# A feed-forward up projection by block products: seven per pair of feature tiles where there were eight, with the gated values kept in DRAM

## The chip, the cores and the metric

The program runs on one core of a Trainium2 chip. The core has a matrix engine (TensorE, PE in the profile), three engines for elementwise work (VectorE or DVE, ScalarE or ACT, GpSimd or POOL), an engine that only issues transfers (SyncE, SP), and 16 DMA engines between its on-chip memory (SBUF) and DRAM. TensorE writes to eight accumulator banks (PSUM), which ACT and DVE read. The metric is the device time of one execution in microseconds (us).

## The reference

Two blocks of a network on 1024 tokens of 1024 features, float32. The part that the change touches is the gated feed-forward layer of the first block, with 2816 hidden features:

```
def conv_glu_ffn(h, w_up, conv_w, w_down):
    up = causal_dwconv(h @ w_up, conv_w)
    ...
    return (jax.nn.silu(gate) * val) @ w_down
```

Here `h` is the normalised input (1024 tokens by 1024 features), `w_up` has 5632 columns (2816 for the gate, then 2816 for the value), `causal_dwconv` is a convolution of three taps along the tokens for each feature, and `w_down` brings 2816 features back to 1024.

## The kernel before

Every float32 operand of a product is split in two parts: `hi`, the rounded value in TensorE's fast format (a cast on ACT, L100), and `lo`, the rest (a subtraction on DVE or GpSimd, L101). A product is then three: hi by hi, hi by lo, lo by hi. The helper `split` writes both parts, `wload` (L103) loads 128 columns of a weight into the tile `wraw` (two buffers) and splits them, and `mm3` multiplies (L123).

The up projection works on 22 pairs of feature tiles (`NF` = 22, 128 features each). A pair is one gate tile and the value tile of the same number; here it is called a unit. For each of the two tiles of a unit the kernel loads 512 KB of weights, splits them, and issues 8 (slices of the 1024 inputs) x 3 (parts) x 2 (halves of the tokens) = 48 products of 128x128 by 128x512: 96 for the unit, 2112 in all. The sums of a tile lie in a PSUM tile `mm` of two banks, one bank for each half of the tokens. `up_evict` (L1030 to L1036) reads it: ACT takes the last tap, DVE the other two (L1034, L1035). Then come tanh on ACT (L1055), two products on DVE (L1056, L1060), and the gated values stay in SBUF, in the tiles `slots`, for the down projection. A new `wraw` can be filled when its older contents are split, so SP's transfer waits for DVE's subtraction.

The down projection (L1165 to L1167) runs in four passes: for each half of the tokens (`j`) and each half of the 1024 output features (`c`) it takes 22 steps, and a step multiplies one 128x512 tile of `w_down` and one of the gated values, split on the way, in 12 products.

A scheduler in the compiler orders the instructions of every engine by priorities and estimated lengths; pools with few buffers set what waits for what. What the scheduler made of the code is shown below with the change.

## Time and profile before

| | us |
|---|---|
| three timed executions | 2518.94, 2516.62, 2511.92 |
| their median | 2516.62 |
| the profiled execution: span from first to last instruction | 2505.2 |
| output projection and norm, from 1020 | 1020.0 to 1110.7 |
| up projection | 1110.7 to 1593.2 |
| down projection | 1593.2 to about 1842 |
| second block | 1842 to 2505.2 |

The span is what the rows below are counted in; the time of an execution also has a start and an end in it, and the median stands 11.4 us above the span (the profiled execution's own time is not listed beside the three). A row of the profile's table of windows gives, for each engine, its busy time and the number of its instructions in that stretch; "PEclk" is the clock that TensorE was granted, as a share of full speed. A busy PE is not the same as a PE that does new work at its full rate, since matmuls are pipelined: the time from the start of one matmul to the start of the next is the price of one.

### The profile page before, as it was taken

To read this page: it belongs to the slowest core of one execution; us is meant where nothing else is said; L and a number is where in the kernel's file an instruction comes from. 1 tells how busy PE (TensorE), PEld (TensorE's weight loads), DVE (VectorE), ACT (ScalarE), POOL (GpSimd) and SP (SyncE) were. 2 spreads that over 40 slices of the span, in tenths; PEclk is the share of its full clock that TensorE was granted. 3 is DMA by queue.
4 is the path that set the end of the run, shared out by engine and by line. 5 is a ranking of instruction groups with operands and counts; after the bars stand their busy time and mean duration, and the time that the engine had idled before them with its cause. 6 is when DMAs were issued, how large, how long until landed. Compare 5 with 4: busy or idle time off the path is not lost.

```text
span 2505.2 us, 31186 instructions
## 1 busy us (share of the span) xinstructions
PE 2396.7 (96%) x11582; PEld 1942.4 (78%) x11582; DVE 1322.8 (53%) x2247; ACT 992.9 (40%) x1869; POOL 356.4 (14%) x477
## 2 busy tenths in 40 slices
PE   6999999997999999999999999999999999999999
PEld 5777777776777777788788888888889787777787
DVE  4244754677554333444444444456665534668852
ACT  4333433222343122323222222345556633669840
POOL 0122320112231211000000000000013200125510
...
GB/s 150 101 88 78 43 58 164 147 147 83 88 119 65 166 153 168 206 77 51 53 50 43 51 51 47 114 97 135 163 125 83 143 179 175 197 187 183 127 107 138
DMA packets 272056, 288.10 MB, mean 115 GB/s; under 512 B 13968, under 2 KB 208160, under 8 KB 271904
## 3 DMA queue, kind: packets, MB, share of 16 engines
...
## 4 chain that ended last, share of the span: by engine, by line
PE 47%; DMA 6%; ACT 3%; DVE 3%; issue 1%; SPq 0%; POOL 0%; POOLq 0%; ACTq 0%; DVEq 0%
PE mm L123 19%; PE ip L1219 3%; DMA mr<-merged 2%; PE tp L330 1%; PE iq L314 1%; PE ip L1108 1%; PE ip L1109 1%; PE ip L1110 1%; PE lt L1503 1%; PE iq L315 1%; ACT p L1507 1%; DMA wr<-in_w_in_dram 1%; PE ho L1503 1%; DMA zr<-in_w_in_dram 1%; PE iq L1109 1%
## 5 line engine op out<-in xcount | busy, mean ns | idle before, releaser
L100 ACT CAST whi<-wraw 128x1024 fp32r<-128x1024 f32 (+1 forms) x138 | 121.8, 883 | 524.8 <-PE mm L123 499.7
L101 DVE TENSOR_TENSOR wlo<-wraw,whi 128x1024 fp32r<-128x1024 f32 (+1 forms) x138 | 143.8, 1043 | 345.6 <-ACT whi L100 341.6
L123 PE MATMUL mm<-hh,whi 128*128 128x512 f32 x896 | 306.4, 413 | 6.0 <-ACT th L846 5.1
L123 PE MATMUL mm<-hl,whi 128*128 128x512 f32 x896 | 293.7, 399 | 0.0
L123 PE MATMUL mm<-hh,wlo 128*128 128x512 f32 x896 | 291.7, 397 | 1.3 <-DVE wlo L115 1.3
L123 PE MATMUL mm<-h2l,whi 128*128 128x512 f32 x704 | 222.4, 389 | 0.0
L123 PE MATMUL mm<-h2h,wlo 128*128 128x512 f32 x704 | 222.0, 389 | 0.0
L123 PE MATMUL mm<-h2h,whi 128*128 128x512 f32 x704 | 222.0, 389 | 0.0
L123 PEld LDWEIGHTS mm<-hh,wlo 128*128 128x128 f32 x896 | 170.6, 191 | 39.2 <-DVE wlo L115 1.9
L123 PEld LDWEIGHTS mm<-hl,whi 128*128 128x128 f32 x896 | 170.3, 191 | 37.2 <-issue 1.0
L123 PEld LDWEIGHTS mm<-hh,whi 128*128 128x128 f32 x896 | 160.9, 192 | 42.1 <-ACT th L846 6.4
L123 PEld LDWEIGHTS mm<-h2l,whi 128*128 128x128 f32 x704 | 132.1, 188 | 28.6 <-issue 1.3
L123 PEld LDWEIGHTS mm<-h2h,whi 128*128 128x128 f32 x704 | 132.1, 188 | 27.9 <-ACT whi L100 0.6
L123 PEld LDWEIGHTS mm<-h2h,wlo 128*128 128x128 f32 x704 | 132.2, 188 | 27.4
L167 POOL TENSOR_TENSOR rs<-rs,negh 128x1 f32<-128x1 f32 x32 | 19.4, 610 | 868.7 <-ACT junk L164 602.9
L1507 ACT ACTIVATE p<-p,mn 128x640 f32<-128x640 f32 (+7 forms) x128 | 99.5, 778 | 12.6 <-DVE mn L1505 12.2
L101 DVE TENSOR_TENSOR gl<-s,gh 128x512 fp32r<-128x512 f32 x87 | 59.8, 689 | 65.4 <-ACT gh L100 62.9
L101 DVE TENSOR_TENSOR ptl<-tp,pth 128x512 fp32r<-128x512 f32 (+3 forms) x144 | 77.9, 554 | 30.7 <-ACT pth L100 29.4
L100 ACT CAST gh<-s 128x512 fp32r<-128x512 f32 x87 | 53.9, 621 | 79.7 <-PE iq L1166 32.7
L100 ACT CAST pth<-tp 128x512 fp32r<-128x512 f32 (+3 forms) x144 | 66.9, 477 | 43.5 <-PE tp L330 42.3
L314 PE MATMUL iq<-pth,v 128*128 128x512 f32 x192 | 70.8, 370 | 9.9 <-ACT pth L100 4.9
L856 POOL TENSOR_TENSOR acc<-acc,pacc 128x1024 f32<-128x1024 f32 x20 | 49.3, 2464 | 186.5 <-DVE acc L851 133.0
...
## 6 DMA issues: line engine op xcount, KB each, us to landing
wraw<-in_w_in_dram SPq DMA_DIRECT2D x60, 512.0 KB, 3.9
wraw<-in_w_up_dram SPq DMA_DIRECT2D x44, 512.0 KB, 3.8
wr<-in_w_down_dram SPq DMA_DIRECT2D x87, 256.0 KB, 2.6
merged<-acc SPq DMA_DIRECT2D x28, 512.0 KB, 2.9
pacc<-merged SPq DMA_DIRECT2D x20, 512.0 KB, 3.9
x<-x ACTq DMA_DIRECT2D x16, 512.0 KB, 2.8
v2t<-vo ACTq DMA_DIRECT2D x16, 512.0 KB, 2.6
v<-v2t SPq DMA_DIRECT2D x16, 512.0 KB, 4.0
```

The lines of the kernel that those rows point to most:

```text
L100: S.copy(hi, src)
L101: (eng or V).tensor_tensor(lo, src, f(hi), op=ALU.subtract)
L123: PE.matmul(ps[:, c0 + j * 512:c0 + (j + 1) * 512], w[:, k, :], x[j][:, k, :], start=(k == 0 and w is wh and x is xh), stop=(k == nkt - 1 ...
L314: PE.matmul(po[-1][:, w], vh[:, k, :], ph_[:, w], start=(k == 0), stop=False)
L315: PE.matmul(po[-1][:, w], vh[:, k, :], pl_[:, w], start=False, stop=(k == nk - 1))
L330: PE.transpose(pt[:, i * 128:(i + 1) * 128], P[p0 + i][:, k * 128:(k + 1) * 128], ident)
L856: G.tensor_tensor(ac, ac, pa, op=ALU.add)
L1108: PE.matmul(ps[:, :ncol], xh[:, k, :], wh[:, :ncol], start=(k == 0), stop=False)
L1109: PE.matmul(ps[:, :ncol], xh[:, k, :], wl[:, :ncol], start=False, stop=False)
L1219: PE.matmul(ps[j], w[:, k, :], x[j][:, n, :], start=(n == 0 and w is wh and x is hh), stop=(n == 7 and bool(last)))
L1503: PE.matmul(ps[:, 0:c1 - c0], a[:, i * 128:(i + 1) * 128], b[:, c0:c1], start=(n == 0), stop=(n == len(self.passes) - 1))
L1507: S.activation(pr_[:, :L], pr_[:, :L], AF.Exp, scale=-1.0, bias=mn[:, c:c + 1], accum_out=self.den[:, i:i + 1])
```

## The change

The normalised input, turned (features by tokens), is seen as four blocks: two halves of the features by two halves of the tokens. A unit's weights are four blocks as well: two halves of the inputs by gate and value. The product of such 2x2 blocks takes eight block products; Strassen's algorithm (here in Winograd's form) takes seven and some more additions. `Unit.p1` to `Unit.p7` are the seven, 4 slices x 3 parts = 12 matmuls each, 84 for a unit and 1848 in all.

- On the side of the tokens, the sums of blocks are made once (lines L1181 to L1197 of the new kernel): `B1` (two blocks as they are), `T1` to `T4` and `B22`, from the raw transposes that `NormBlocks` keeps; each of `T1` to `T4` and `B22` is 128x2048 and split in `hi` and `lo`.
- On the side of the weights, four sums of 128x512 are made for each unit on GpSimd (`sums`, L1070 to L1073), from both `wraw` tiles. They make two tiles `s12` and `s34` of 128x1024, each split (`pair`) into `uhi` and `ulo`. The gate's weights are split as before (`w1`), and of the value's only the lower half (`w4`, 128x512).
- The products of one unit are added up in two accumulator banks of one `mm` tile (`a` and `c`) and one bank of `ip` (`d`). What several outputs share is read out between products: `e1` (ACT's copy of `a` after `p1`), `u2` and `e15` (DVE). The gate's and value's columns before the convolution are now in SBUF (`cg`, `cx`): `c11` is ACT's copy of `a`, the other three quarters are DVE additions (L1134, L1138, L1142). The convolution (`conv`) reads these.
- The last product of the gate is made on GpSimd (L1159, 128x1024), and the result is written to DRAM (`gg_d`, 512 KB for a unit). The down projection loads it again in its first two passes, 44 tiles of 256 KB (L1337).
- The small tables of the second block, which stood in the fifth turn of the loop, stay in the fifth (`n == 4`). Pools change sides; outside the feed-forward layer every engine runs the same instructions in the same order.

The diff, cut to its core:

```diff
+    class NormBlocks(Norm):
+        def __init__(self, pool, psum, gain, parts, raws):
+            super().__init__(pool, psum, gain, None, None)
+            self.parts, self.raws = parts, raws
+        def turn(self, t, xn):
+            j, c = divmod(t, 4)
+            s = slice(c * 128, (c + 1) * 128)
+            for q in range(2):
+                pt = self.psum.tile([128, 512], F32, name="tp", bufs=2).rearrange("p (a b) -> p a b", a=4)
+                for i in range(4):
+                    PE.transpose(pt[:, i, :], xn[q][:, i * 128:(i + 1) * 128], ident)
+                S.copy(self.raws[q, j][:, :, s], pt)
+                if j == 0:
+                    hi, lo = self.parts[q]
+                    split(hi[:, :, s], lo[:, :, s], self.raws[q, j][:, :, s])
...
+    gg_d = dram.tile([NF * 128, T], F32, name="gg")
+    stu = ExitStack()
+    up = None
+    def halves4(x):
+        return x[:, 0:4, :], x[:, 4:8, :]
+    class Unit:
+        def __init__(self, fi):
+            self.fi = fi
+        def load(self):
+            self.raw = [wpool.tile([128, NK, 128], F32, name="wraw") for _ in range(2)]
+            for i in range(2):
+                c = (i * NF + self.fi) * 128
+                nc.sync.dma_start(self.raw[i], A["w_up"][:, c:c + 128].rearrange("(k p) c -> p k c", p=128))
+        def w1(self):
+            hi = wpool.tile([128, NK, 128], F32R, name="whi")
+            lo = wpool.tile([128, NK, 128], F32R, name="wlo")
+            split(hi, lo, self.raw[0])
+            (self.a11, self.a12) = zip(halves4(hi), halves4(lo))
+        def sums(self):
+            (a11, a12), (a21, a22) = map(halves4, self.raw)
+            x = up.tile([128, 2, 4, 128], F32, name="s12")
+            y = up.tile([128, 2, 4, 128], F32, name="s34")
+            G.tensor_tensor(x[:, 1], a21, a22, op=ALU.add)
+            G.tensor_tensor(x[:, 0], x[:, 1], a11, op=ALU.subtract)
+            G.tensor_tensor(y[:, 0], a11, a21, op=ALU.subtract)
+            G.tensor_tensor(y[:, 1], a12, x[:, 0], op=ALU.subtract)
+            self.x, self.y = x, y
+        def pair(self, x):
+            hi = up.tile([128, 2, 4, 128], F32R, name="uhi", bufs=2)
+            lo = up.tile([128, 2, 4, 128], F32R, name="ulo", bufs=2)
+            split(hi, lo, x)
+            return (hi[:, 0], lo[:, 0]), (hi[:, 1], lo[:, 1])
+        def w2(self):
+            self.s2, self.s1 = self.pair(self.x)
+        def w3(self):
+            self.s3, self.s4 = self.pair(self.y)
+        def w4(self):
+            hi = wpool.tile([128, NK, 128], F32R, name="whi")[:, 0:4, :]
+            lo = wpool.tile([128, NK, 128], F32R, name="wlo")[:, 0:4, :]
+            split(hi, lo, self.raw[1][:, 4:8, :])
+            self.a22 = hi, lo
+        def product(self, acc, w, x, start):
+            (wh, wl), (xh, xl) = w, x
+            for k in range(4):
+                for n, (a, b) in enumerate(((wh, xh), (wh, xl), (wl, xh))):
+                    PE.matmul(acc, a[:, k, :], b[:, k, :], start=(start and k + n == 0), stop=(k == 3 and n == 2),
+                              skip_group_check=True)
+        def banks(self):
+            ps = mmp.tile([128, T], F32, name="mm")
+            self.a, self.c = ps[:, 0:512], ps[:, 512:1024]
+        def p1(self):
+            self.product(self.a, self.a11, B1[0], True)
+            self.e()
...
+        def e(self):
+            self.e1 = up.tile([128, 512], F32, name="e1", bufs=2)
+            S.copy(self.e1, self.a)
+        def p2(self):
+            self.product(self.a, self.a12, B1[1], False)
+        def c11(self):
+            self.g = up2.tile([128, T], F32, name="cg")
+            S.copy(self.g[:, 0:512], self.a)
+        def p6(self):
+            self.product(self.c, self.s2, T2, True)
+            self.u2 = up.tile([128, 512], F32, name="u2")
+            V.tensor_tensor(self.u2, self.c, self.e1, op=ALU.add)
+        def p5(self):
+            self.d = ipx.tile([128, 512], F32, name="ip", bufs=2)
+            self.product(self.d, self.s1, T1, True)
+            self.e15 = up.tile([128, 512], F32, name="e15")
+            V.tensor_tensor(self.e15, self.d, self.e1, op=ALU.add)
+        def p7(self):
+            self.product(self.c, self.s3, T3, False)
+            self.v = up2.tile([128, T], F32, name="cx")
+            V.tensor_tensor(self.v[:, 512:1024], self.c, self.e15, op=ALU.add)
+        def p3(self):
+            self.product(self.d, self.s4, B22, False)
+            V.tensor_tensor(self.g[:, 512:1024], self.d, self.u2, op=ALU.add)
+        def p4(self):
+            self.product(self.c, self.a22, T4, False)
+            V.tensor_tensor(self.v[:, 0:512], self.c, self.e1, op=ALU.add)
+        def conv(self, x, w):
+            a = up2.tile([128, T], F32, name="cv", bufs=3)
+            S.activation(a, x, AF.Copy, scale=w[2])
+            V.scalar_tensor_tensor(a[:, 1:T], x[:, 0:T - 1], w[1], a[:, 1:T], op0=ALU.mult, op1=ALU.add)
+            V.scalar_tensor_tensor(a[:, 2:T], x[:, 0:T - 2], w[0], a[:, 2:T], op0=ALU.mult, op1=ALU.add)
             return a
-        for fi in range(NF):
...
-                    mm3(ps[i], *w2[i], hh, hl, NK)
-                    cv_.append(up_evict(ps[i], i * NF + fi))
...
+        def gate(self):
+            a = self.conv(self.g, [PV("ffn_conv_w", 2 * NF * i + self.fi) for i in range(3)])
+            self.th = up2.tile([128, T], F32, name="th")
+            S.activation(self.th, a, AF.Tanh, scale=0.5)
+            V.scalar_tensor_tensor(self.th, self.th, 1.0, a, op0=ALU.add, op1=ALU.mult)
+        def value(self):
+            b = self.conv(self.v, [vw[:, NF * i + self.fi:NF * i + self.fi + 1] for i in range(3)])
+            G.tensor_tensor(b, self.th, b, op=ALU.mult)
+            nc.sync.dma_start(gg_d[self.fi * 128:(self.fi + 1) * 128, :], b)
+    us = [Unit(fi) for fi in range(NF)]
+    us[0].load()
+    us[0].w1()
+    us[0].banks()
+    us[0].product(us[0].a, us[0].a11, B1[0], True)
+    last_turn()
+    sto.close()
+    up = stu.enter_context(tc.tile_pool(name="up", bufs=1, side="right", reuse_waits="tile"))
+    vw = up.tile([128, 3 * NF], F32, name="vw")
+    tc.keep_in_program_order(V.tensor_scalar(vw.rearrange("p (i f) -> p i f", i=3),
+                                             PV("ffn_conv_w", 0, 6 * NF).rearrange("p (i e f) -> p i e f", i=3, e=2)[:, :, 1, :],
+                                             0.5, None, op0=ALU.mult))
+    tpool = stu.enter_context(tc.tile_pool(name="tpool", bufs=1, side="right", reuse_waits="tile"))
+    T4, T1, T2, T3, B22 = [[tpool.tile([128, 4, 512], F32R, name=f"{n}{e}") for e in "hl"] for n in ("t4", "t1", "t2", "t3", "b2")]
+    us[0].e()
+    us[0].p2()
+    us[0].sums()
+    us[0].w2()
+    V.tensor_tensor(R2[0, 0], R2[0, 1], R2[0, 0], op=ALU.subtract)
+    split(*T1, R2[0, 0])
+    split(*B22, R2[1, 1])
+    G.tensor_tensor(R2[0, 1], R2[1, 1], R2[0, 1], op=ALU.subtract)
+    us[0].w4()
+    us[1].load()
+    us[1].w1()
+    us[1].banks()
+    us[1].p1()
+    us[1].p2()
+    V.tensor_tensor(R2[1, 1], R2[1, 1], R2[0, 0], op=ALU.subtract)
+    split(*T2, R2[1, 1])
+    us[0].p5()
+    us[0].w3()
+    V.tensor_tensor(R2[1, 0], R2[1, 0], R2[1, 1], op=ALU.subtract)
+    split(*T3, R2[0, 1])
+    split(*T4, R2[1, 0])
+    str_.close()
+    up2 = stu.enter_context(tc.tile_pool(name="up2", bufs=1, reuse_waits="tile"))
+    us[0].c11()
+    us[1].sums()
+    us[0].p6()
+    us[1].w2()
+    us[0].p3()
+    us[0].gate()
+    us[0].p7()
+    us[1].w3()
+    us[0].p4()
+    us[0].value()
+    us[1].w4()
+    us[2].load()
+    us[1].p5()
+    us[1].c11()
+    us[1].p6()
+    us[2].w1()
+    us[2].sums()
+    us[1].p3()
+    us[1].gate()
+    us[1].p7()
+    us[2].w2()
+    us[1].p4()
+    us[1].value()
+    us[2].w3()
+    for n in range(2, NF):
+        u, v = us[n], us[n + 1] if n < NF - 1 else None
+        u.banks()
+        u.p1()
+        u.w4()
+        if v:
+            v.load()
+        u.p6()
+        if n == 4:
+            with tc.tile_pool(name="tb", bufs=1) as tb:
+                block2_tables(tb)
+        u.p5()
+        u.p2()
+        u.c11()
+        if v:
+            v.w1()
+            v.sums()
+        u.p7()
+        if v:
+            v.w2()
+        u.p3()
+        u.gate()
+        u.p4()
+        u.value()
+        if v:
+            v.w3()
...
+                    if j == 0:
+                        g_ = f(slot(c))
+                        nc.sync.dma_start(g_, gg_d[fi * 128:(fi + 1) * 128, c * 512:(c + 1) * 512])
+                        gg.setdefault(fi, {})[c] = g_
+                    raw = dw.tile([128, 512], F32, name="wr", bufs=3)
+                    nc.sync.dma_start(raw, A["w_down"][fi * 128:(fi + 1) * 128, c * 512:(c + 1) * 512])
+                    wh, wl, gh, gl = [dw.tile([128, 512], F32R, name=name, bufs=2) for name in ("dwh", "dwl", "gh", "gl")]
+                    with tc.high_priority():
+                        split(wh, wl, raw)
+                        split(gh, gl, gg[fi][j])
```

What the scheduler makes of it is shown at three places. The first is a unit in the middle of the up projection, on ACT and on GpSimd. ACT before (`whi` the cast of a weight tile, `cv` the first tap of the convolution, `th` tanh):

```order
L100 CAST whi_9859<-wraw_9857 128x1024
L1033 ACTIVATE cv_9840<-mm_9739,pv_63 128x1024
L100 CAST whi_9978<-wraw_9976 128x1024
L1033 ACTIVATE cv_9913<-mm_9863,pv_63 128x1024
L1055 ACTIVATE th_9969<-cv_9913 128x1024
```

ACT after, from the copy `e1` of unit n (its PSUM tile is mm_9793) to the copy `e1` of unit n+1:

```order
L1111 COPY e1_9806<-mm_9793 128x512
L100 CAST uhi_9883<-s12_9863 128x1024
L100 CAST whi_9859<-wraw_9812 128x1024
L1118 COPY cg_9857<-mm_9793 128x512
L100 CAST uhi_9926<-s34_9864 128x1024
L1146 ACTIVATE cv_9900<-cg_9857,pv_63 128x1024
L100 CAST whi_9945<-wraw_9813 128x512
L1146 ACTIVATE cv_9920<-cx_9881,vw_8203 128x1024
L1154 ACTIVATE th_9904<-cv_9900 128x1024
L1111 COPY e1_9943<-mm_9930 128x512
```

Five instructions for each unit have become nine, and `c11` of unit n (L1118) stands behind two casts that belong to unit n+1 (`uhi` of `s12`, and `whi`). The product `p7` of unit n waits for that copy, since `a` and `c` lie in one tile and the wait is placed for the tile. GpSimd, which has no instruction of the feed-forward layer before, has these for the same unit (wraw_9812 and wraw_9813 are the weights of unit n+1, cv_9783 is the value of unit n-1):

```order
L1070 TENSOR_TENSOR s12_9863<-wraw_9813 128x512
L1159 TENSOR_TENSOR cv_9783<-th_9767,cv_9783 128x1024
L1071 TENSOR_TENSOR s12_9863<-s12_9863,wraw_9812 128x512
L1072 TENSOR_TENSOR s34_9864<-wraw_9812,wraw_9813 128x512
L1073 TENSOR_TENSOR s34_9864<-wraw_9812,s12_9863 128x512
```

The product with the gate (L1159) stands between the first and the second sum of the next unit's weights.

The second place is DVE at the start of the up projection. Before, there stand (after the last splits of the norm) the small tables and the first unit:

```order
L101 TENSOR_TENSOR wlo_8305<-wraw_8302,whi_8304 128x1024
L1034 SCALAR_TENSOR_TENSOR cv_8287<-mm_8189,pv_63,cv_8287 128x1023
L1035 SCALAR_TENSOR_TENSOR cv_8287<-mm_8189,pv_63,cv_8287 128x1022
L1056 SCALAR_TENSOR_TENSOR th_8295<-th_8295,cv_8287 128x1024
L101 TENSOR_TENSOR wlo_8311<-wraw_8308,whi_8310 128x1024
```

After, the operands `T1` to `T4` and `B22` (names t1l to t4l, b2l, and the raw blocks r00 to r11) are made there:

```order
L101 TENSOR_TENSOR ulo_8306<-s34_8233,uhi_8305 128x1024
L1181 TENSOR_TENSOR r00_7415<-r01_7416,r00_7415 128x2048
L101 TENSOR_TENSOR b2l_8217<-r11_7418,b2h_8216 128x2048
L101 TENSOR_TENSOR t1l_8211<-r00_7415,t1h_8210 128x2048
L101 TENSOR_TENSOR wlo_8257<-wraw_8252,whi_8256 128x1024
L1191 TENSOR_TENSOR r11_7418<-r11_7418,r00_7415 128x2048
L101 TENSOR_TENSOR t3l_8215<-r01_7416,t3h_8214 128x2048
L101 TENSOR_TENSOR t2l_8213<-r11_7418,t2h_8212 128x2048
L1129 TENSOR_TENSOR e15_8303<-ip_8290,e1_8218 128x512
L1195 TENSOR_TENSOR r10_7417<-r10_7417,r11_7418 128x2048
L101 TENSOR_TENSOR wlo_8402<-wraw_8253,whi_8401 128x512
L101 TENSOR_TENSOR t4l_8209<-r10_7417,t4h_8208 128x2048
```

Eight subtractions of 128x2048 stand ahead of the second unit's work; the small tables follow them.

The third place is SP at the end of the up projection. Before, the transfers of the down projection's weights stand behind the last loads of the up projection, and one of them (L1064) between:

```order
L107 DMA wraw_10732<-in_w_up_dram 128x8x128
L1064 DMA wraw_10851<-in_w_down_dram 128x512
L107 DMA wraw_10864<-in_w_up_dram 128x8x128
L107 DMA wraw_10870<-in_w_up_dram 128x8x128
L1153 DMA wr_11023<-in_w_down_dram 128x512
```

After (gg is the buffer in DRAM, cv_11272 the gated values of the last unit, x2 the rows of the residual, s0 the tiles that the down projection reads):

```order
L1340 DMA wr_11358<-in_w_down_dram 128x512
L1364 DMA x2_11840<-x1_7408 128x1024
L1364 DMA x2_11842<-x1_7408 128x1024
L1340 DMA wr_11382<-in_w_down_dram 128x512
L1364 DMA x2_11844<-x1_7408 128x1024
L1340 DMA wr_11406<-in_w_down_dram 128x512
L1160 DMA gg_8164<-cv_11272 128x1024
L1364 DMA x2_11846<-x1_7408 128x1024
L1337 DMA s0_11305<-gg_8164 128x512
L1337 DMA s0_11329<-gg_8164 128x512
```

The first load of gated values (the tile of unit 0) stands in the queue behind the store of the last unit's.

## Rows read from the trace of the kernel before

**Rows 1.** The profile's table of windows, by stage.

```profile
core 0: us, PE busy (x) PEld busy (x) DVE busy (x) ACT busy (x) POOL busy (x), PEclk, DMA share, GB/s
1020.00:1110.70 90.70, 84.61 (x390) 67.48 (x389) 43.20 (x64) 29.91 (x57) 3.86 (x7) 1.00 0.42 140
1110.70:1593.20 482.50, 482.50 (x2127) 397.38 (x2126) 219.83 (x214) 117.46 (x119) 0.55 (x1) 1.00 0.16 48
1593.20:1842.00 248.80, 247.26 (x1092) 201.02 (x1091) 155.96 (x246) 129.05 (x244) 6.59 (x9) 1.00 0.43 139
```

**Rows 2.** The waits of the up projection: engine, line, waited for; us, times, longest.

```profile
ACT whi L100 <- PE mm L123: 276.3, 41, 11.7
DVE wlo L101 <- ACT whi L100: 213.3, 41, 6.7
```

**Rows 3.** The timeline of PE inside a unit: start, us, what, count.

```profile
1200.07 0.62 PE L123 MATMUL mm<-h2l,whi 128*128 128x512 f32 x2
...
1202.34 0.62 PE L123 MATMUL mm<-h2h,whi 128*128 128x512 f32 x2
```

**Rows 4.** The timeline of the other engines around one weight tile.

```profile
1288.33 1.05 ACT L100 CAST whi<-wraw 128x1024 fp32r<-128x1024 f32 x1 [4.90 <-PE mm L123]
1289.28 1.11 ACT L1033 ACTIVATE cv<-mm,pv 128x1024 f32<-128x1024 f32 x1
1289.42 1.23 DVE L101 TENSOR_TENSOR wlo<-wraw,whi 128x1024 fp32r<-128x1024 f32 x1 [4.73 <-ACT whi L100]
1290.56 1.28 DVE L1034 SCALAR_TENSOR_TENSOR cv<-mm,pv,cv 128x1023 f32<-128x1023 f32 x1
1290.67 0.37 SPq L107 DMA_DIRECT2D wraw<-in_w_up_dram  x1
```

**Rows 5.** Groups by shape in the up projection (count, busy us, mean ns, idle before).

```profile
L101 DVE TENSOR_TENSOR wlo<-wraw,whi 128x1024 fp32r<-128x1024 f32 x42 | 51.4, 1225 | 213.3 <-ACT whi L100 213.3
L1060 DVE SCALAR_TENSOR_TENSOR s<-th,cv 128x512 f32<-128x512 f32 x42 | 27.2, 688 | 0.7
L100 ACT CAST d<-wraw 128x512 fp32r<-128x512 f32 x1 | 0.6, 622 | 3.7 <-DMA wraw<-in_w_down_dram 3.7
```

**Rows 6.** Groups by shape on GpSimd, elsewhere in the kernel.

```profile
L101 POOL TENSOR_TENSOR fol<-wr,foh 128x512 fp32r<-128x512 f32 x8 | 10.2, 1292 | 4.3 <-ACT foh L100 3.9 <-DMA raw<-mk 0.4
L101 POOL TENSOR_TENSOR ml<-mr,mh 128x1024 fp32r<-128x1024 f32 x4 | 9.6, 2396 | 0.2 <-ACT mh L100 0.2
```

**Rows 7.** The page's transfers: KB each, median us from issue to landing.

```profile
wraw<-in_w_up_dram SPq DMA_DIRECT2D x44, 512.0 KB, 3.8
wr<-in_w_down_dram SPq DMA_DIRECT2D x87, 256.0 KB, 2.6
```

**Rows 8.** The same list, for the up projection alone: the small tables.

```profile
oh<-in_onehot_dram ACTq DMA_DIRECT2D x3, 48.0 KB, 1.7
```

**Rows 9.** The timeline of GpSimd and DVE where both read two SBUF operands at once.

```profile
460.30 1.22 DVE L632 SCALAR_TENSOR_TENSOR kk<-kk,lw 128x1024 f32<-128x1024 f32 x1
461.29 2.48 POOL L634 TENSOR_TENSOR a__3175<-a__3175,cu 128x1024 f32<-128x1024 f32 x1 [5.77 <-ACT cu L624]
461.44 3.42 DVE L636 TENSOR_TENSOR k__3123<-k__3123,cu 128x1024 f32<-128x1024 f32 x1
...
863.23 1.22 DVE L101 TENSOR_TENSOR wlo<-wraw,whi 128x1024 fp32r<-128x1024 f32 x1
863.38 2.20 POOL L827 TENSOR_TENSOR ab<-ab 128x512 f32<-128x512 f32 x1 [6.80 <-DVE ab L825]
```

**Rows 10.** The timeline of both where DVE reads one operand from PSUM (tp).

```profile
2306.10 1.30 POOL L1535 TENSOR_TENSOR t<-t,zz 128x512 f32<-128x512 f32 x1
...
2306.72 0.69 DVE L101 TENSOR_TENSOR ptl<-tp,pth 128x512 fp32r<-128x512 f32 x1
```

**Rows 11.** The timeline at the start and at the end of the up projection.

```profile
1110.48 0.39 PE L951 MATMUL ip<-h,ml 128*128 128x512 f32 x1
...
1110.90 0.69 DVE L953 TENSOR_TENSOR x<-x,ip 128x512 f32<-128x512 f32 x1 [3.99 <-PE ip L951]
```

**Rows 12.** The timeline where the first product of the down projection follows.

```profile
1593.00 0.39 PE L123 MATMUL mm<-h2h,wlo 128*128 128x512 f32 x1
...
1593.22 0.39 PE L1165 MATMUL ip<-d,d 128*128 128x512 f32 x1
```

**Rows 13.** The table of windows: the busiest transfers, and PE after a pause.

```profile
1016.00:1022.00 6.00, 6.00 (x28) 4.95 (x28) 2.57 (x5) 1.34 (x3) 0.00 (x0) 1.00 1.01 366
...
590.00:600.00 10.00, 0.00 (x0) 0.00 (x0) 9.79 (x8) 0.00 (x0) 0.75 (x3) 0.51 0.00 0
600.00:610.00 10.00, 9.36 (x57) 7.42 (x58) 7.16 (x22) 3.63 (x11) 9.04 (x22) 0.80 0.27 82
...
10.00:20.00 10.00, 4.04 (x18) 2.86 (x17) 5.01 (x10) 5.65 (x13) 1.75 (x3) 1.00 0.87 286
```

More of the change, by code (lines that the diff above doesn't have):

```diff
@@ L922 @@
     h2pool = st2.enter_context(tc.tile_pool(name="h2pool", bufs=1, reuse_waits="tile"))
+    str_ = ExitStack()
+    h2raw = str_.enter_context(tc.tile_pool(name="h2raw", bufs=1, reuse_waits="tile"))
+    R2 = {(q, j): h2raw.tile([128, 4, 512], F32, name=f"r{q}{j}") for q in range(2) for j in range(2)}
     wo1 = sto.enter_context(tc.tile_pool(name="wo1", bufs=1, reuse_waits="tile"))
-    hh = [h2pool.tile([128, NK, 512], F32R, name=f"h2h{j}") for j in range(2)]
-    hl = [h2pool.tile([128, NK, 512], F32R, name=f"h2l{j}") for j in range(2)]
-    nm = Norm(wo1, ipx, A["ffn_norm_g"], hh, hl)
+    B1 = [[h2pool.tile([128, 4, 512], F32R, name=f"b{q}{e}") for e in "hl"] for q in range(2)]
+    nm = NormBlocks(wo1, ipx, A["ffn_norm_g"], B1, R2)
     x1s, M = {}, {}
@@ L969 @@
         turn = nxt
-    turn()
-    sto.close()
-    if stop == 3:
-        nc.sync.dma_start(out, x1_d)
-        st2.close()
-        return
+    last_turn = turn
     st3 = ExitStack()
-    slots = st3.enter_context(tc.tile_pool(name="slots", bufs=NF, side="right"))
-    def slot(j, ncol=512):
-        return slots.tile([128, 512], F32R, name=f"s{j}")[:, :ncol]
     u_d = dram.tile([8, NU], F32, name="u2")
@@ L1070, with slot @@
+    stu.close()
     st2.close()
     stw.close()
+    slots = st3.enter_context(tc.tile_pool(name="slots", bufs=NF, reuse_waits="tile"))
+    def slot(j, ncol=512):
+        return slots.tile([128, 512], F32R, name=f"s{j}")[:, :ncol]
+    gg = {}
     x3_d = dram.tile([T, D], F32, name="x3")
     sth = ExitStack()
-    h3pool = sth.enter_context(tc.tile_pool(name="h3pool", bufs=1, reuse_waits="tile"))
+    h3pool = sth.enter_context(tc.tile_pool(name="h3pool", bufs=1, side="right", reuse_waits="tile"))
@@ L1137 @@
     nm, xs = None, []
-    with tc.tile_pool(name="dw", bufs=1, reuse_waits="tile") as dw:
+    with tc.tile_pool(name="dw", bufs=1, side="right", reuse_waits="tile") as dw:
         rows_ = [[lambda k=k: Wc.append(row2(dw, A["w_in_2"], 0, 2048, 416, k, 3)) for k in range(NK)]
@@ L1148 @@
                 for fi in range(NF):
[L1149 to L1157 removed]
+                    if j == 0:
[8 more added lines that the diff above has]
+                        split(gh, gl, gg[fi][j])
                     if (j, c, fi) == (0, 0, 1):
[L1159 to L1160 removed]
+                        dn = std.enter_context(tc.tile_pool(name="dn", bufs=1, reuse_waits="tile"))
                     if j and c:
@@ L1227, in gate_pair @@
         yield
-    ibw = st3.enter_context(tc.tile_pool(name="ibw", bufs=1, reuse_waits="tile"))
+    ibw = st3.enter_context(tc.tile_pool(name="ibw", bufs=1, side="right", reuse_waits="tile"))
     def rope(dst, src, t, nh):
@@ L1387 @@
             std.close()
-            ibl = st3.enter_context(tc.tile_pool(name="ibl", bufs=1, side="right", reuse_waits="tile"))
+            ibl = st3.enter_context(tc.tile_pool(name="ibl", bufs=1, reuse_waits="tile"))
         if u != "c" and u not in W:
@@ L1418 @@
     sta = ExitStack()
-    at = sta.enter_context(tc.tile_pool(name="at", bufs=1, side="right", reuse_waits="tile"))
-    zw = sth.enter_context(tc.tile_pool(name="zw", bufs=1, reuse_waits="tile"))
+    at = sta.enter_context(tc.tile_pool(name="at", bufs=1, reuse_waits="tile"))
+    zw = sth.enter_context(tc.tile_pool(name="zw", bufs=1, side="right", reuse_waits="tile"))
     cm = []
@@ L1587 @@
     stf = ExitStack()
-    fo = stf.enter_context(tc.tile_pool(name="fo", bufs=1, reuse_waits="tile"))
+    fo = stf.enter_context(tc.tile_pool(name="fo", bufs=1, side="right", reuse_waits="tile"))
     for h in range(NG, 16):
@@ L1617 @@
     sta.close()
-    with tc.tile_pool(name="fp", bufs=1, side="right", reuse_waits="tile") as fp:
+    with tc.tile_pool(name="fp", bufs=1, reuse_waits="tile") as fp:
         def out_x(t, c):
```

48 lines of the change are left out of this document (removed).

## The prediction

> **What bounds the kernel now.** I read the windows by stage first. In the up projection PE is busy for the whole 482.50 us [rows 1], DVE for 220, ACT for 117, and the transfers take 0.16 of their engines. The table of waits says the same from the other side: the largest waits are ACT's and DVE's, and they are for PE or for each other in step with PE [rows 2]; no row has PE waiting for a weight. So the stage is as long as its matmuls: 482.50 / 2127 = 0.2268 us each, which the timeline repeats (ten matmuls between 1200.07 and 1202.34, 0.227 each) [rows 3]. A unit takes 482.5 / 22 = 21.93 us. There is no gap to the down projection: its first product starts 0.22 us after the last of the up projection [rows 12], since its operands lie ready.
>
> **What is removed.** 264 matmuls by 0.2268 are 59.9 us, if PE stays the bound. A unit of 84 would take 19.05 us. Whether it can is decided by what has to be made ready for the next unit inside that time.
>
> **A unit in the middle.** `wraw` still has two buffers, and a unit now needs both at once until its last split (`w4`). The next unit's second tile (the one that GpSimd needs first) is therefore loaded only after DVE's `lo` of `w4`. From there a ring of waits leads through all engines back to the same point. Its links, in order:
> - load of 512 KB: 3.85 (3.8 to landing [rows 7], and the wait's end);
> - GpSimd: the first sum 1.29, the product L1159 of 128x1024 2.40, the second sum 1.29 [rows 6], together 4.98;
> - ACT: `uhi` of `s12` and `whi`, each start 0.95 after the one before [rows 4], then `c11` to its end 0.62 [rows 5]: 2.52;
> - PE: `p7` has waited for `c11` and starts some 0.1 behind it. 17 matmuls (`p7`, and the five of `p3` that are left) are 16 x 0.2268 from the first start to the last, and 0.42 on to a reader [rows 11]: 4.15;
> - `uhi` of `s34` reuses a buffer that `p3` reads, so it starts there: ACT 1.05 [rows 4];
> - DVE, in its order: `ulo` 1.14, a tap of the gate 1.14, the value's quarter (L1142) 0.61, the other tap 1.14, and `lo` of `w4` 0.69. (Starts of 1024 wide ones are 1.14 apart [rows 4], 0.08 less than one takes; 512 wide ones take 0.69 [rows 5], so 0.61.) Together 4.72.
>
> The sum is 3.85 + 4.98 + 2.52 + 4.15 + 1.05 + 4.72 = **21.3**. That is above 19.05: PE does not bound the unit any more. It waits some 2.2 us in each, at `p7`, and a unit costs 21.3 where it cost 21.93. Over 18 units in the steady part this gives back 18 x 0.63 = 11.3 us of the 59.9. Each of some 14 joints may be off by 0.05, so 20.6 to 22.0 bound it: -24 to +1.
>
> [...]
>
> **The start.** DVE gets eight instructions of 128x2048 (the second place shown with the change). No row has the shape. From 0.69 for 512 and 1.225 for 1024 [rows 5], each further 512 costs 0.535, so 2.30; the bound above is twice 1.225. 8 x 2.30 = 18.4. With the two `ulo`, `wlo`, the small `wlo` and `e15` it is 18.4 + 3 x 1.23 + 2 x 0.69 = 23.5 us in a row, from about 1115.2 (after `p1` of unit 0, `e1`, and `uhi`). GpSimd has, in the same stretch, four sums of 1.29 and L1184 of 128x2048 (4.6, by the same step from rows 6), about 10 us, and DVE's `r11` (L1191) waits for the last.
>
> Do these lie beside each other? The rows say no. Where both engines read two operands from SBUF the one that starts second stands until the first is done: GpSimd's 512 takes 2.20 in place of 1.29 when `wlo` started 0.15 ahead of it, and DVE's subtraction of 1024 takes 3.42 in place of 1.22 when GpSimd's 2.48 started 0.15 ahead [rows 9]. Where DVE reads one operand from PSUM, neither is longer (1.30 and 0.69) [rows 10]. All of DVE's instructions above but `e15` read two from SBUF. So the two add up: 1115.2 + 23.5 + 10.0 = 1148.7. [...]
>
> Behind them ACT issues the small tables' transfers (1.7 to 1.8 [rows 8]), DVE takes four small steps and `u2` (1.9), and `p7` of unit 0 starts at 1152.4. 96 matmuls are left to the end of `p1` of unit 2: 21.8, and some 4 us of waits where DVE or GpSimd hold each other up again: 1178. Before, the same point is 1110.7 + 2 x 21.93 + 2.7 = 1157.3. So **+21**; unit 2 still waits for its own late second load, 24.1 for 21.9: **+2.2**. Bounds: +8 (the engines side by side) to +28. PE is busy for over half of this; at 10 to 20 us it was busy for 4 of 10 at full clock, and only the idle 590 to 600 brought 0.51 and then 0.80 [rows 13], so I put no clock in.
>
> In the steady unit the same exclusion costs nothing by my sum: GpSimd's last two sums and DVE's `ulo` and `wlo` push each other, 1.1 to 1.3 us each, but there are 6 us until `s34` is needed. The nearest miss is at the load's landing: DVE's last tap ends about 0.4 us ahead of it.
>
> **The end.** The last unit has no successor and no gap: from the end of its `p1` 72 matmuls are left, 16.3 us, where 84 were, 84 / 96 x 21.93 = 19.2: **-2.9**. Then PE stands. After `p4` comes: reader 0.42, quarter 0.69, first tap on ACT 1.06, tap on DVE 1.14, a split of the weights 0.61, the product with tanh 1.14, a split 0.61, last tap 1.22, GpSimd 2.40, and only then SP, whose queue holds the first load of `gg` behind that store; landing 2.6 [rows 7] or somewhat more beside the store and residual rows (1 MB), say 2.9; cast 0.62 and start 0.1. **+12.9** where it was 0.
>
> **The down projection** loads 44 more tiles. Its first two passes then move 58 tiles of 256 KB, 15.2 MB; the trace shows 366 GB/s at best [rows 13], so 41.5 us for some 49 us of PE if all comes at once in the first pass. I take no cost; above it, +5, and +20 if the queue runs at the half.
>
> **Sum:** 21 + 2.2 - 11.3 - 2.9 + 12.9 = **+21.9 us**. On the span of 2505.2 that is 2527.1; on the median of 2516.6, which lies 11.4 above it, **2538.5**.
>
> **The rivals.**
> 1. PE stays the bound, since the ring is shorter than I have it (a link that overlaps). At 19.3 the 18 units give back 47, not 11.3: 2502, **faster**. It decides from a ring of 19.7 on (29 us less over 18 units: the 21.9 and 7.5 more). For it: the joints are taken from single rows. Against: it needs 1.6 us less, and the load, GpSimd and the matmuls alone, 12.5 us, have rows of the same shapes.
> 2. DVE and GpSimd run side by side at the start: 14.5 less, 2524, near the bound of no difference. Against: rows 9.
> 3. The ring is longer: DVE's last tap lies ahead of GpSimd's first sum and holds it, 1.1 us for each of 18 units: 2558. For it: a margin of only 0.4.
> 4. The loads of `gg` starve the first pass: 2543 to 2558. Against: 41.5 below 49.
> [...]
>
> **How the numbers follow.** This kernel's runs lie 0.3% apart, so 0.3% (7.5 us) is what can be told. Forecast 0.60 (2526 to 2548 alone), rival 1 0.10, rival 2 0.10 (half of it no difference), rival 3 0.10, rival 4 0.08, rival 5 0.02. Slower 0.79, same 0.11 (half of rival 2, the low edge of the forecast and weak cases of rival 1), faster 0.10. The range leaves out rival 1 and the far parts of 3 and 4: 2516 to 2556.
>
> **What would show it.** Each unit in the middle 21.3 us, with PE idle before one `p7` matmul in each, put down to ACT L1118; SP's load waiting for DVE L101; DVE rows over 2 us for 1024 at the start; first L1351 about 13 us behind the last L1098. It is wrong if PE has no gap in the middle, or if the matmuls themselves are slower than 0.227.

## The result and the profile after

The changed kernel takes 2545.57 us (median of four executions, 2540.20 to 2549.54); the kernel before, run beside it, takes 2515.19 (four executions, 2511.92 to 2518.94). The ratio is 1.011, with a 95% interval of 1.0089 to 1.0131: about 30 us slower. The time was inside the range, 7 us above the forecast.

The profiled execution has a span of 2547.8 us, 42.6 more than the profile before. Not all of it is the change: the first product of the up projection starts at 1119.58, where it was 1110.70. Up to about 1003 VectorE executes the same instructions in the same order in both kernels, and the last of them already starts 10.0 later (1013.31 for 1003.28); from there to the first product the orders differ a little. In the seven experiments below the first product lies anywhere from 1106.4 to 1120.5, so I take the 8.9 us for the difference of two executions. The windows by stage hold the rest (columns as in [rows 1]):

```profile
1020.00:1119.58 99.58, 94.65 (x435) 75.92 (x434) 44.78 (x63) 36.16 (x69) 10.60 (x12) 1.00 0.48 151
1119.58:1636.16 516.58, 451.91 (x1863) 350.07 (x1861) 350.99 (x336) 188.15 (x213) 192.44 (x108) 0.96 0.24 76
1636.16:1886.00 249.84, 248.70 (x1090) 202.69 (x1091) 151.00 (x241) 127.22 (x242) 6.26 (x8) 0.99 0.53 168
```

The up projection, to the first product of the down projection, is 516.58 us for 482.50. PE, which was busy for all of it [rows 1], now has 264 products less and stands for 64.7 us. The down projection is 249.84 for 248.80. I measure the stage at the same points in every run below: e1(n), the start of ScalarE's copy behind `p1` of unit n, and for the kernel before the same place in its row of matmuls.

| from, to | before | after | difference | forecast |
|---|---|---|---|---|
| first product to e1(2) | 46.6 | 68.8 | +22.2 | +21 |
| e1(2) to e1(3) | 21.9 | 26.4 | +4.5 | +2.2 |
| 18 units, e1(3) to e1(21) | 18 x 21.93 | 18 x 21.59 | -6.1 | -11.3 |
| e1(21) to the first down product | 19.2 | 32.7 | +13.5 | -2.9 + 12.9 |
| sum | 482.5 | 516.6 | +34.1 | +21.9 |

**The steady unit.** The table of waits from 1110 to 1650 has PE waiting for ScalarE's copy `c11` once in a unit, which it never did before [rows 2]:

```profile
POOL s L1070 <- DMA wraw<-in_w_up_dram: 239.1, 18, 14.7
ACT uhi L100 <- POOL s L1071: 150.0, 19, 8.2
PEld mm L1098 <- ACT cg L1118: 39.4, 21, 2.8
PE mm L1098 <- ACT cg L1118: 30.5, 19, 2.4
```

The chain that ended last, followed back from 1366 to 1343, is one turn of the ring (start, us, what):

```profile
1342.90 0.61 DVE wlo L101
...
1343.53 3.86 DMA wraw<-in_w_up_dram
...
1347.56 0.10 POOL s L1070
...
1348.81 2.39 POOL cv L1159
1351.20 1.26 POOL s L1071
...
1352.48 0.02 ACT uhi L100
...
1353.43 1.04 ACT whi L100
1354.47 0.49 ACT cg L1118
...
1355.01 3.06 PE mm L1098 x12
1358.07 0.95 PE ip L1098 x4
...
1359.10 1.06 ACT uhi L100
...
1361.32 1.28 DVE cv L1147
...
1363.11 1.27 DVE cv L1148
1364.39 0.61 DVE wlo L101
...
1365.02 3.70 DMA wraw<-in_w_up_dram
```

Read it by the starts. Load to first sum 1343.53 to 1347.56, 4.03 (forecast 3.85); GpSimd to 1352.48, 4.92 (4.98); ScalarE to 1355.01, 2.53 (2.52); PE and its reader to 1359.10, 4.09 (4.15); then `uhi` and VectorE to the next load 1365.02, 5.92 (1.05 + 4.72). The turn is 21.49 where the sum said 21.3: no link is off by more than 0.2.

**The start.** The timeline of VectorE and GpSimd in the first 30 us:

```profile
1126.34 3.38 DVE L1181 TENSOR_TENSOR r<-r,r 128x2048 f32<-128x2048 f32 x1
1127.64 3.21 POOL L1071 TENSOR_TENSOR s<-s,wraw 128x512 f32<-128x512 f32 x1
1129.64 3.36 DVE L101 TENSOR_TENSOR b2l<-r,b2h 128x2048 fp32r<-128x2048 f32 x1
1130.81 3.31 POOL L1072 TENSOR_TENSOR s<-wraw 128x512 f32<-128x512 f32 x1
...
1142.97 2.29 DVE L1191 TENSOR_TENSOR r<-r,r 128x2048 f32<-128x2048 f32 x1 [4.49 <-POOL r L1184]
```

Alone, a 128x2048 instruction takes 2.29 (the estimate was 2.30). Beside GpSimd it takes 3.36, 1.07 more, and GpSimd's sums of 128x512, 1.29 alone, take 3.2 to 3.3. They pass one after the other: the first four rows end at 1129.72, 1130.85, 1133.00 and 1134.12, by turns VectorE's and GpSimd's.

**The end.** The timeline behind the last product:

```profile
1626.96 2.34 POOL L1159 TENSOR_TENSOR cv<-th,cv 128x1024 f32<-128x1024 f32 x1 [17.86 <-issue]
1629.33 0.32 SPq L1160 DMA_DIRECT2D gg<-cv  x1
1629.69 0.43 SPq L1364 DMA_DIRECT2D x<-x  x1
1630.17 7.00 SPq L1337 DMA_DIRECT2D s<-gg  x11
1635.49 1.30 ACT L100 CAST gh<-s 128x512 fp32r<-128x512 f32 x2 [11.54 <-DMA s<-gg]
...
1636.16 0.80 PE L1351 MATMUL ip<-dwh,gh 128*128 128x512 f32 x1 [16.45 <-ACT gh L100]
```

From the end of the product, 1629.30, to the cast are 6.2 us, where the forecast put 2.9: the first load is issued 0.9 later, behind the store and a residual row, and takes 5.3 from there. The order is as forecast: product on GpSimd, store, and only then the loads, the first of which holds a tile written long before.

### The profile page after: what moved, and what is told of

Read it like the earlier page. It is cut to its first block, busy times and chain, and to the rows that moved or that the text cites. A ratio compares the mean times of both kernels' runs of the same rounds, so it can differ in the third digit from the quotient of the medians.

```text
span 2547.8 us, 31230 instructions
## 1 busy us (share of the span) xinstructions
PE 2378.5 (93%) x11318; PEld 1906.3 (75%) x11318; DVE 1447.7 (57%) x2358; ACT 1067.1 (42%) x1970; POOL 553.0 (22%) x588
## 4 chain that ended last, share of the span: by engine, by line
PE 30%; DMA 6%; DVE 5%; issue 5%; ACT 5%; POOL 3%; SPq 0%; ACTq 0%; POOLq 0%; DVEq 0%
PE mm L1098 3%; PE ip L1405 3%; DMA wraw<-in_w_up_dram 3%; POOL cv L1159 2%; PE ip L1294 1%; PE ip L1295 1%; PE ip L1296 1%; PE tp L349 1%; PE iq L333 1%; DVE cv L1147 1%; PE iq L334 1%; PE lt L1689 1%; DVE cv L1148 1%; PE ip L1098 1%; POOL s L1071 1%
## 5 line engine op out<-in xcount | busy, mean ns | idle before, releaser
L101 DVE TENSOR_TENSOR wlo<-wraw,whi 128x1024 fp32r<-128x1024 f32 (+2 forms) x138 | 153.9, 1117 | 133.4 <-ACT whi L100 129.5
L100 ACT CAST whi<-wraw 128x1024 fp32r<-128x1024 f32 (+2 forms) x138 | 112.1, 813 | 267.4 <-PE mm L123 223.3
L100 ACT CAST uhi<-s 128x1024 fp32r<-128x1024 f32 x44 | 46.1, 1050 | 239.9 <-POOL s L1071 150.0
L101 DVE TENSOR_TENSOR ulo<-s,uhi 128x1024 fp32r<-128x1024 f32 x44 | 56.7, 1291 | 74.6 <-ACT uhi L100 74.5
L1070 POOL TENSOR_TENSOR s<-wraw 128x512 f32<-128x512 f32 x22 | 29.4, 1335 | 278.6 <-DMA wraw<-in_w_up_dram 239.1
L349 PE MATMUL tp<-cv,p 128*128 128x128 f32 x432 | 71.2, 275 | 1.5 <-DVE ptl L101 1.4
L403 DVE TENSOR_TENSOR_SCAN ex<-kp,zero 128x128 f32<-128x128 f32 (+7 forms) x32 | 43.5, 1360 | 46.1 <-POOL kp L399 46.1
L334 PE MATMUL iq<-ptl,v 128*128 128x512 f32 x192 | 68.8, 364 | 0.0
```

The lines of the kernel that those rows point to most:

```text
L100: S.copy(hi, src)
L101: (eng or V).tensor_tensor(lo, src, f(hi), op=ALU.subtract)
L334: PE.matmul(po[-1][:, w], vh[:, k, :], pl_[:, w], start=False, stop=(k == nk - 1))
L349: PE.transpose(pt[:, i * 128:(i + 1) * 128], P[p0 + i][:, k * 128:(k + 1) * 128], ident)
L403: V.tensor_tensor_scan(ex[:, 0:L][:, ::-1], kp[:, :L][:, ::-1], zero1.to_broadcast([128, L]), 1.0, ALU.mult, ALU.add)
```

## The experiments

All seven were timed beside the kernel before. Ratios are to it.

**1. The copy `c11` ahead of the next unit's casts.** PE's wait at `p7` is for `c11`, which stands on ScalarE behind two casts for the next unit that wait for a load and for GpSimd. Here those casts may be issued only after `c11`; nothing is removed. Behind `c11`, `whi` now also comes ahead of `uhi` on ScalarE, and `wlo` ahead of `ulo` on VectorE.

```diff
-            S.copy(self.g[:, 0:512], self.a)
+            self.c11_ = S.copy(self.g[:, 0:512], self.a).ins
...
-            v.w1()
-            v.sums()
+            with tc.issue_after(u.c11_):
+                v.w1()
+                v.sums()
         u.p7()
         if v:
-            v.w2()
+            with tc.issue_after(u.c11_):
+                v.w2()
```

> In every unit from the third on, ACT's copy of the first quarter (c11) is put ahead of the two casts of the next unit; nothing else is moved. Theory of the ring (one unit is as long as the chain load, GpSimd, ACT, p7, p3, DVE, load): p7 no longer waits, the ring loses its ACT and PE links, and the next longest path through the same engines sets the unit, about 19.9 us in place of 21.5: 18 to 19 units, 25 to 30 us less than the changed kernel, about 2518, no gap before p7. Rival (the unit is as long as what DVE and GpSimd exclude each other for): ACT's order does not matter, the unit stays 21.5 and the time 2546.

Measured: 2514.4 us, ratio 0.9993 (0.9974 to 1.0013): the whole loss is gone. The steady unit is 19.93. e1(2) is at +68.7 and the end is 32.5, as in the changed kernel; the unit between e1(2) and e1(3) is 24.0, where it was 26.4. In the table of waits from 1214 to 1570 ScalarE now waits for PE with `c11`, and PE itself no more for it:

```profile
ACT cg L1118 <- PE mm L1098: 135.9, 18, 8.5
...
PEld mm L1098 <- DVE cx L1134: 10.3, 17, 0.8
```

So PE is the bound again, but for 0.6 us a unit that its weight load waits for VectorE's addition behind `p7`. The ring is shown: one link cut, and the unit falls by 1.66 us, to what PE takes.

**2. A second pair of `wraw` buffers.** Every second unit's weights go to a pool of their own, from unit 7 on, so that a load need not wait for the last split of the unit before.

```diff
-            self.raw = [wpool.tile([128, NK, 128], F32, name="wraw") for _ in range(2)]
+            pool = uw[0] if uw and self.fi % 2 else wpool
+            self.raw = [pool.tile([128, NK, 128], F32, name="wraw") for _ in range(2)]
...
                 block2_tables(tb)
+            uw.append(stu.enter_context(tc.tile_pool(name="uw", bufs=2, reuse_waits="tile")))
```

> From unit 5 on every other unit takes its two weight tiles from a second pair of buffers, so that a unit is loaded a whole unit earlier; on GpSimd the product with the gate then comes ahead of the sums. Theory of the ring: the load (3.9) is out of it, units 7 to 21 take about 20.1 in place of 21.5, some 17 to 20 us less than the changed kernel, about 2527. Rival (exclusion of DVE and GpSimd sets the unit): no change, 2546, GpSimd's first sum no longer waits for a load and the unit stays 21.5.

Measured: 2523.8 us, ratio 1.0029 (1.0009 to 1.0050); from there the unit is 20.1, and the stage is 492.7 in all. In the table of waits from 1214 to 1570 the first sum (L1071 here) waits for a load twice, before the pool is in use, and from then on for VectorE:

```profile
POOL s L1071 <- DMA wraw<-in_w_up_dram: 25.5, 2, 13.4
POOL s L1071 <- DVE ulo L101: 17.0, 14, 1.2
```

The ring opens at the load as well. The scheduler also put the product with the gate ahead of both sums here, so load and product left the ring together, and the run does not tell them apart.

**3. The start on one engine.** Unit 1's four sums and the difference L1184 go from GpSimd to VectorE.

```diff
         def sums(self):
+            G = V if self.fi == 1 else nc.gpsimd
...
-    G.tensor_tensor(R2[0, 1], R2[1, 1], R2[0, 1], op=ALU.subtract)
+    V.tensor_tensor(R2[0, 1], R2[1, 1], R2[0, 1], op=ALU.subtract)
```

> Unit 1's four sums of weights and the one 128x2048 difference that GpSimd makes at the start are made on DVE. Theory (at the start the two engines exclude each other, so their times add up, and GpSimd is the slower): 10 us of GpSimd become 5 of DVE, unit 2 starts about 8 us earlier, 2538. Rival (they ran side by side): DVE, which is the chain there, has 5 us more work, so 4 to 5 us more, 2550.

Measured: 2540.85 us, ratio 1.0093 (1.0063 to 1.0124). e1(2) is at +59.8, 9.0 us earlier, and the stage is 509.9, 6.7 less than in the changed kernel: its steady units are 21.83 on average, with three that take 23.3. The time alone can't be told from the changed kernel's (2545.57, ratio 1.0089 to 1.0131); the reading rests on the trace. The timeline of VectorE shows why more work on it ends sooner:

```profile
1124.39 2.29 DVE L1182 TENSOR_TENSOR r<-r,r 128x2048 f32<-128x2048 f32 x1
1126.59 2.29 DVE L101 TENSOR_TENSOR b2l<-r,b2h 128x2048 fp32r<-128x2048 f32 x1
1128.80 2.29 DVE L101 TENSOR_TENSOR t1l<-r,t1h 128x2048 fp32r<-128x2048 f32 x1
1131.00 2.29 DVE L1185 TENSOR_TENSOR r<-r,r 128x2048 f32<-128x2048 f32 x1
```

Nothing is stretched any more, and L1185, the moved difference, takes 2.29 where GpSimd took 5.58 with VectorE idle for 4.49 of it. GpSimd's work had not been beside VectorE's; it was between: 4.3 us of VectorE's time in the changed kernel are the four instructions that were stretched, by 1.05 to 1.09 each, and 4.49 the wait for L1184. (The scheduler put the four sums behind the last split.)

**4. The gate's last product on VectorE.** L1159 leaves GpSimd, where it stood between the two sums of the ring.

```diff
-            G.tensor_tensor(b, self.th, b, op=ALU.mult)
+            V.tensor_tensor(b, self.th, b, op=ALU.mult)
```

> The product of gate and value (128x1024) is made on DVE in every unit. Theory of the ring: GpSimd's 2.4 us leave it, but DVE's extra 1.2 us come into the part between p3 and the next load: 20.9 in place of 21.5 for a unit, and 1 to 2 us less at the end, 10 to 13 us less in all, about 2535. Rival (PE or anything off DVE and GpSimd bounds the unit): no change, 2546.

Measured: 2537.97 us, ratio 1.0077 (1.0050 to 1.0103); the steady unit is 20.96, 0.63 less, and the stage 504.7. The interval of the time overlaps that of the changed kernel; the unit is what shows the edit. It is a smaller change than the 2.40 us taken out of GpSimd's part of the ring, for two reasons. The product of 1.23 now stands on VectorE just where the load lands, and the first sum waits for it. And the third sum, L1072, has moved up into the product's place, 1.25 from start to start. GpSimd in one unit, and a group of this run, 1214 to 1570:

```profile
1398.66 1.29 POOL L1072 TENSOR_TENSOR s<-wraw 128x512 f32<-128x512 f32 x1
1399.90 1.28 POOL L1071 TENSOR_TENSOR s<-s,wraw 128x512 f32<-128x512 f32 x1
...
L1070 POOL TENSOR_TENSOR s<-wraw 128x512 f32<-128x512 f32 x17 | 31.2, 1835 | 260.0 <-DMA wraw<-in_w_up_dram 260.0
```

1.84 for 1.29, and 2.40 - 1.25 - 0.55 are 0.60 of the 0.63. The stretched first sum is what my third rival said of the changed kernel itself. There the last tap ends 0.5 us ahead of the landing, and the same sum has 1.294 over 18.

**5. Two loads past the store.** The first two loads of gated values are issued from ScalarE's queue instead of SyncE's.

```diff
-                        nc.sync.dma_start(g_, gg_d[fi * 128:(fi + 1) * 128, c * 512:(c + 1) * 512])
+                        (S if c == 0 and fi < 2 else nc.sync).dma_start(g_, gg_d[fi * 128:(fi + 1) * 128, c * 512:(c + 1) * 512])
```

> The end alone: the first two loads of gated values that the down projection takes are issued from ScalarE's queue, where they don't stand behind the last unit's 512 KB store on SyncE's. Theory (the end's extra is the landing of the last two transfers one after the other, in one queue): the first down matmul comes some 5 us earlier than after's 32.7 us behind e1(21), so about 27.5, the steady unit stays 21.6, and the time is about 2540, 5 us under the changed kernel. Rival (the load waits for the store's data, not for the queue): e1(21) to the first down matmul stays 32 to 33 and the time stays at 2545.

Measured: e1(21) to the first down product 27.96 for 32.66, about the 27.5 expected. The timeline, by the start of the issue, the cast and the product:

```profile
1627.33 3.92 ACTq L1337 DMA_DIRECT2D s<-gg  x2
...
1632.05 0.32 SPq L1160 DMA_DIRECT2D gg<-cv  x1
...
1633.52 0.62 ACT L100 CAST gh<-s 128x512 fp32r<-128x512 f32 x1 [6.85 <-DMA s<-gg]
1634.19 0.79 PE L1351 MATMUL ip<-dwh,gh 128*128 128x512 f32 x1 [11.75 <-ACT gh L100]
```

The cast starts 1.5 us after the last store was issued, for 6.2 in the changed kernel, so the load had waited for its place in the queue, not for the store. The first load does not reach its cast quicker: from its issue at 1627.33 to the cast are 6.2 us (5.3 in the changed kernel), with no store ahead of it in ScalarE's queue (a 512 KB transfer was issued there 2.5 us before); the view of the transfers from 1626 to 1636 has 4.0 as the median landing of the two. It only starts earlier. So the run does not show that the landing is long because of the store in the same queue, as my theory had it. The time, 2543.63, ratio 1.0097 (1.0059 to 1.0134), can't tell 4.7 us from none: its interval holds that of the changed kernel.

**6. The three together.** Experiments 1, 3 and 5 in one kernel; no new edit (unit 1's sums are four; the text on record says three).

> Three edits together: the next unit's casts wait for c11's copy (first experiment), unit 1's three sums and one difference on VectorE (third), two loads of gated values from ScalarE's queue (fifth). If the three losses are separate, as I put them: e1(2) some 9 us earlier than in after (+60 instead of +69 from the first product), steady unit 19.9, end near 27, so from the first product to the first down matmul about 484 - 9 - 5 = 470, against 482.5 in before: a time near 2502, 12 to 14 us under before. Rival (the start's and the end's gain are taken back by the ring or by the clock): 484 again and a time near 2515, the same as before.

Measured: 2500.34 us, ratio 0.9938 (0.9915 to 0.9961), faster than both kernels. e1(2) at +59.5, the steady unit 19.93, the end 27.9. One forecast in it was off: the unit after e1(2) takes 25.5 and not 24, so the stage is 471.8 for the 470 expected:

```profile
1116.77:1588.60 471.83, 446.03 (x1864) 348.62 (x1862) 348.49 (x341) 188.79 (x213) 166.38 (x103) 0.97 0.25 81
```

The three losses are separate and add up: 516.6 - 32.6 (ring) - 9.0 (start) - 4.7 (end) would be 470.3. In the unit that was off, nine products from 1195.66 to 1199.30 start 0.405 apart at a granted clock of 0.53, where 0.233 is usual; that is 1.5 us, the size of what is left.

**7. The operands' address.** PE's own share was larger than forecast. In all these runs matmuls whose moving operand is one of `t1` to `t4` or `b2` take longer than those with `b0` and `b1` (medians of 395 to 397 ns for 389 in the changed kernel, 1220 to 1500). By the sizes of the tiles ahead of them theirs begin at another offset within 64 bytes, as I work it out; no trace shows an address. Here the three edits stay, and those tiles move by 32 bytes.

```diff
-    vw = up.tile([128, 3 * NF], F32, name="vw")
+    vw = up.tile([128, 3 * NF + 8], F32, name="vw")[:, 0:3 * NF]
```

> The same three edits, and the ten operand tiles t1 to t4 and b2 moved down by 32 bytes, so that they begin at the same offset within 64 bytes as the tiles of B1 (b0, b1), which stream at 0.2268 us a matmul where t1 to t4 and b2 stream at 0.2333 to 0.2371. If the address sets the pace: the 60 matmuls of a unit come to 0.2268 too, the steady unit falls from 19.9 to 19.5, and the time is some 8 us under the kernel with the three edits. Rival (the pace hangs on what else runs beside the products, or on which PSUM bank they write): the pace stays at 0.233 or more and the time is within 3 us of the kernel with the three edits.

Measured: 2497.34 us, ratio 0.9933 (0.9909 to 0.9957), not to be told from experiment 6; the steady unit is 19.95. The tile `mm` in experiment 6, 1300 to 1500 (ns minimum/median/maximum):

```profile
L1099 PE MATMUL mm<-b1h,wlo x40: 388/389/390, 1307.7 to 1488.7; 128*128 128x512 f32 x40
L1099 PE MATMUL mm<-t3h,ulo x40: 392/396/397, 1311.4 to 1492.4; 128*128 128x512 f32 x40
```

and in this one, 1220 to 1500:

```profile
L1099 PE MATMUL mm<-b1h,wlo x57: 388/390/394, 1220.1 to 1498.7; 128*128 128x512 f32 x57
L1099 PE MATMUL mm<-t3h,ulo x56: 393/394/399, 1221.7 to 1482.5; 128*128 128x512 f32 x56
```

No tile's median moves by more than 4 ns, and `t3h` is still behind `b1h`; the unit is the same. Two groups remain, with starts 0.233 and 0.229 apart, and the unit did not gain. The move by 32 bytes does not set the unit, and my theory falls.

## Why the prediction was right

**PE stops being the bound: right.** The gap is where it was put, before one `p7` product in each unit and behind `c11`, and experiments 1, 2 and 4 cut or shorten the ring at three links, with the unit falling to 19.9, 20.1 and 21.0. Rival 1, PE staying the bound, is excluded by the gap. Of the 59.9 us that 264 products are worth, the ring let through 6.1.

**The ring's length: 21.3 for 21.59.** The mechanism was right, the term mis-sized: 18 x 0.63 = 11.3 was to come back, and 6.1 did. Of the 5.2 us, 18 x 0.19 = 3.4 are the joints (21.49 in the turn shown: load and landing 0.18, VectorE 0.15, the others within 0.07), and 1.7 is one unit of 23.24 in which the granted clock fell: behind a gap before `p7`, eight products start 0.424 apart at a granted clock of 0.50 (1463.49 to 1466.88). The forecast's own second sign of being wrong, matmuls slower than 0.227, did appear (0.233 for 60 of a unit's 84), but only 17 of them lie in the ring, 0.1 us. That the exclusion costs nothing in the steady unit was right: the groups from 1214 to 1603 have the two that push each other at 1.0 to 1.1 over their price, and neither is in the turn (the `wlo` there is the unit's other one, of 128x512):

```profile
L101 DVE TENSOR_TENSOR wlo<-wraw,whi 128x1024 fp32r<-128x1024 f32 x18 | 41.5, 2307 | 0.0
L1073 POOL TENSOR_TENSOR s<-wraw,s 128x512 f32<-128x512 f32 x18 | 41.0, 2279 | 0.0
```

**The start: +21 for +22.2.** The estimate for 128x2048 and the exclusion held, and VectorE's last split of the start, which the sum had at 1148.7, ended 1157.6 in an execution that began 8.9 later. That it came out to the tenth is luck: 2.2 us in which VectorE waits for ScalarE's casts stood in no term, 128x2048 instructions start 2.20 apart and not 2.30, and the stretches and the wait for L1184 are 8.8 (given with experiment 3) where 10.0 were added. The 1.2 that it is over lie behind: VectorE waits 3.3 us for the small tables' transfer, where the sum had 1.7 to 1.8. Rival 2, side by side, would have been 14.5 us less (by its own terms 14.0: the 10.0, and some 4 of waits); experiment 3, which leaves nothing on GpSimd to exclude, ends 9.0 sooner although VectorE then does five instructions more. One thing stood in no term: "I put no clock in". The clock did fall, with PE pausing before: for up to 5 us in the start, 2.1 and 2.8 us in the unit behind it, and 16.8 us at the end. The windows (the start; inside the unit behind it; the end; the first eleven products of the down projection):

```profile
1119.58:1188.40 68.82, 52.83 (x194) 38.38 (x193) 54.92 (x50) 28.66 (x31) 27.53 (x11) 0.85 0.15 48
1204.00:1207.50 3.50, 3.50 (x10) 2.68 (x10) 2.03 (x2) 0.00 (x0) 0.75 (x1) 0.51 0.27 98
1603.50:1636.16 32.66, 16.21 (x70) 12.49 (x68) 13.74 (x16) 6.05 (x9) 4.74 (x2) 0.81 0.57 195
1636.16:1641.01 4.85, 4.85 (x11) 3.79 (x12) 1.36 (x2) 0.62 (x1) 0.00 (x0) 0.50 1.05 395
```

In the start the slow products cost nothing that shows. The earlier ones lie ahead of pauses of 5.4 and 2.2 us; the last, eight from 1163.24 on, lie where VectorE has no gap (1160.94 to 1184.78), and the product at 1184.84 waits for VectorE's addition L1134. In the unit behind the start, +4.5 for +2.2, it explains 1.5 of the 2.3 us: eight products from 1204.05 to 1207.43 start 0.42 apart. Experiments 2 and 3 have the same two pauses without the slow products, and there the unit takes 24.7; experiment 1, with no pause before `p7`, has 24.0. At the end the clock fell while PE stood (0.62 from 1620.00 to 1636.16, where PE is busy for none of it), and the cost lies behind the joint.

**The end: +13.5 for +10.0.** The chain to GpSimd's product was right: from the start of the last matmul, 1619.32, to its end, 1629.30, are 10.0 us for 9.3 in the sum. The step that failed is the landing, "say 2.9": it was 6.2 with the issue, 5.3 from the issue, which is also the median that the page lists for these loads. Leaving SyncE's queue did not shorten the way of the first load from its issue to its cast (6.2, experiment 5). Why it is twice 2.6 was not separated; what the trace shows beside it is that eleven loads are issued in a row with the store and the residual rows, and that the transfers come to a mean of 343 GB/s over 12 us, near the best of before, 366 [rows 13], as the transfer view from 1626 to 1638 has it:

```profile
DMA packets 1698, 4.12 MB, mean 343 GB/s; under 512 B 183, under 2 KB 183, under 8 KB 1698
```

**The down projection: 0 for +1.0.** The 44 loads don't starve the first passes: behind the first eleven products PE starts 260 more with no wait, 0.227 apart. Rival 4 is excluded. The +1.0 comes from the clock: those eleven take 4.84 us where 2.50 would be usual, 2.3 us more, which the rest of the stage partly makes up. Passing through DRAM costs at the joint alone, and the joint is 2.3 dearer than its row in the table says.

**GpSimd's durations: as in the rows.** In the ring the sums take 1.294 and the product 2.398 (18 each), as [rows 6] had them. No run shows GpSimd quicker there than its rows (rival 5, with its chance of 0.02).

**The time.** The sum was made against the span 2505.2, and I put the median 11.4 above it as if that were a constant. The time of an execution is 1.7 above its span (2549.54 for 2547.8, and the same in the other three), so the profile before came from an execution quicker than all that were timed, and the one after from the slowest of four. The medians differ by 30.4, the profiles by 42.6, the feed-forward layer in them by 35.1. Against that layer the sum of 21.9 is 13.2 short, and every one of its terms came out dearer than forecast; against the medians it is 8.5 short. That the time lies only 7 above the forecast is in part luck: no run says how much of the 35.1 stands in the medians' 30.4.
